# A data-dependent branch that is not taken: at the tail of an expert stage, or behind the first products of its tenth pair

## The chip, the cores and the metric

The kernel runs on one core of a Trainium2 chip. The metric is the device time of one execution in microseconds (us), as a median over runs. The engines named below are PE (TensorE: matmuls, and PEld, its weight loads), ACT (ScalarE), DVE (VectorE), POOL (GpSimd) and SP (SyncE, which here issues the large DMA transfers). Each has its own instruction stream and is synchronized with the others by semaphores. Times on the trace count from the first instruction.

## The reference

Two blocks are run one after the other over 256 tokens of width 1024. The second block has two layers, and each layer ends in a mixture of experts, the place of this change: 32 experts in four groups, two experts chosen for each token.

```
def second_block(x, ...):
    h = layer_norm(x, ln_in_g, ln_in_b)
    for i in range(DEPTH):                      # DEPTH = 2
        mix = hybrid_mixer(h, ...)
        h = layer_norm(DEEPNORM_ALPHA * h + mix, ln1_g[i], ln1_b[i])
        ffn = hierarchical_moe(h, ...)
        h = layer_norm(DEEPNORM_ALPHA * h + ffn, ln2_g[i], ln2_b[i])
    return h

# in grouped_expert_mlp, for each token's two experts e, with gate weight g:
#   y += g * ((silu(x @ w_gate[e]) * (x @ w_up[e])) @ w_down[e])
```

## The kernel before

`moe()` computes the expert stage of one layer. The weights of all 32 experts are read whatever the routing, and each expert has 64 slots (`CAP`) into which its tokens are gathered. The experts are taken in 16 pairs. A loop over `st` from 0 to 17 runs the pairs as a pipeline: at `st` come the gate and up products of pair `st` (`first_products`, L1793), the additions of pair `st-2` into the output's accumulators (`combine`, L1834, in two halves), the transposes of pair `st-1` (`turned`, L1810, evicted by ACT at L1812), the gating of pair `st` (`gated`, L1802 and L1803), on odd `st` the gathering of the tokens of the next pairs (`gather`, L1700 to L1734), and the down products of pair `st-1` (`second_products`, L1820, evicted at L1823 and L1824).

The weights come in 96 transfers of 2 MB a layer, two each for gate, up and down of a pair, into ten places. All stand on SP's queue, in the order of their use; transfer n reuses the place of transfer n-10 and so waits until PE has read that one. Two of the ten places are made of two halves (L1554), one for each expert of the pair; the others are one transfer (L1544).

An expert could be chosen by more tokens than it has slots. The largest count of a layer stands in `mxi` (tile `e_kept`, written before the loop). Every engine loads it into a register (`values_load`, L1856) and jumps over the body of `overflow()` if the count is no larger than 64 (`tc.If`, L1857). With the inputs here it is not larger in either layer: the body is skipped in both. The body's instructions stand in every engine's stream between the compare and the code after it. PE's order is written by hand: the loop's order is kept on PE (`manual_schedule`), and this is interrupted around the branch. The order of the other engines is found by the scheduler, which moves nothing across the branch.

Of the kernel before, what the change touches and what calls it, by code (L numbers as in the profile page):

```python
# [19 lines left out]
S = 256  # L20
# [680 lines left out]
def row_of(k, cols):  # L701

    b = k.t(k.work, [P, D], "row", bufs=3)
    for h in range(2):
        p = k.ps(tag="m3")
        for j in range(4):
            c = 4 * h + j
            k.nc.tensor.matmul(p[:, j * P:(j + 1) * P], cols[:, c:c + 1].to_broadcast([P, P]), k.ident,
                               start=True, stop=True)
        k.nc.scalar.activation(b[:, h * 512:(h + 1) * 512], p, AF.Copy)  # L710
    return b
# [781 lines left out]
CAP = 64  # L1493
NE = 32

EW = (("ew0", 3), ("ew1", 6))

NX, SPLIT = 10, 6
# [2 lines left out]
def moe(k, l, h, hsum, rows, const, cc):  # L1501


    nc, tc, a, W, A = k.nc, k.tc, k.a, k.work, k.act
# [3 lines left out]

    view = {n: k.t(W, [P, m, 2048], n) for n, m in EW}
    view["hx"] = k.t(k.const, [P, 10, 1024], "hl", F32, 1).rearrange("p (a b) c -> p a (b c)", b=2)  # L1510
# [46 lines left out]
    def prefetch(n):  # L1557
        while nxt[0] < min(n, len(order)):
            fetch(nxt[0], (1,) if nxt[0] == SPLIT else (0, 1))
            nxt[0] += 1  # L1560
            if nxt[0] == SPLIT - 2:
                fetch(SPLIT, (0,))
        if n >= len(order):

            while later:
                nc.sync.dma_start(*later.pop(0))
# [8 lines left out]
    G, pos = (kept[:, o:o + 64].rearrange("p (t e) -> p t e", t=NT) for o in (0, 64))  # L1575
# [3 lines left out]
    hH, hL = (k.t(k.act, [P, NT, D], f"e_{n}", F32R) for n in "hl")  # L1579
# [3 lines left out]
    for t in range(NT):  # L1583
# [3 lines left out]
        last = nc.vector.scalar_tensor_tensor(hc[:, t], h[:, t], mean, rows[0], op0=OP.add, op1=OP.mult).ins  # L1587
# [31 lines left out]
    def low_parts(t, after):  # L1619
        with tc.issue_after(after):  # L1620
            return nc.vector.tensor_tensor(hL[:, t], hc[:, t], hH[:, t].bitcast(F32), op=OP.subtract).ins
# [8 lines left out]
    acc = k.acc()  # L1630

    def residual(src, i):
        for t in range(NT):
            for hf in range(2):
                nc.tensor.matmul(acc[t][hf], al[:, i], src[:, t, hf * 512:(hf + 1) * 512],
                                 start=src is hH and i == 0, stop=False)
# [42 lines left out]
    last = low_parts(0, nc.vector.tensor_tensor(v(M), v(M), og4, op=OP.mult).ins)  # L1679
# [9 lines left out]
    sh = k.t(A, [P, 2, 512], "e_sh")  # L1689
# [77 lines left out]
    mxi = kept[:, 128:129].bitcast(I32)  # L1767
# [11 lines left out]
    last = NE // 2 - 1  # L1779

    def first_products(pr, xg, between=None):
        es = (2 * pr, 2 * pr + 1)
        gu = []
        for nm in ("gate", "up"):
            p = k.ps(tag="aux")
            for q in range(2):
                prefetch(index[nm, q, pr] + NX)
                if q and between:
                    between()
                    between = None  # L1790
                for kk, i in steps:
                    o = (es[i] % 4) * CAP
                    nc.tensor.matmul(p[64 * i:64 * i + 64], xg[:, 4 * q + kk, o:o + CAP], tiles[nm, q, pr](i, kk),  # L1793
                                     start=(q == 0 and kk == 0), stop=(q == 1 and kk == 3))
            gu.append(p)
            if pr == 0 and nm == "gate":
                next(first)
        return gu

    def gated(pr, gate, up):  # L1800
        s_ = sh[:, 0]
        nc.scalar.activation(s_, gate, AF.Silu)  # L1802
        i = nc.vector.scalar_tensor_tensor(s_, s_, at[pr][1], up, op0=OP.mult, op1=OP.mult)  # L1803
        k.anchor = s_[:, :1]
        return i.ins

    def turned():
        p = k.ps([P, 4, P], "m3")
        for f in range(4):
            nc.tensor.transpose(p[:, f], sh[:, 0, f * P:(f + 1) * P], k.ident)  # L1810
        hh = sh[:, 1].rearrange("p (f c) -> p f c", f=4)
        nc.scalar.activation(hh, p, AF.Copy)  # L1812
        return hh

    def second_products(pr, hh):
        for hf in range(2):
            p = k.ps(tag="m3")
            prefetch(index["down", hf, pr] + NX)
            for f, i in steps:
                nc.tensor.matmul(p[64 * i:64 * i + 64], hh[:, f, 64 * i:64 * i + 64],  # L1820
                                 tiles["down", hf, pr](i, f), start=f == 0, stop=f == 3)
            yh, yl = ys[:, 2 * hf], ys[:, 2 * hf + 1]
            nc.scalar.activation(yh, p, AF.Copy)  # L1823
            nc.vector.tensor_tensor(yl, p, yh.bitcast(F32), op=OP.subtract)  # L1824

    def combine(pr, hf):
        if pr == -1 and hf == 1:
            residual(hL, 0)
        if pr < 0:
            return  # L1830
        sT, _ = at[pr]
        for t in range(NT):
            for q in range(2):
                nc.tensor.matmul(acc[t][hf], sT[:, t * P:(t + 1) * P], ys[:, 2 * hf + q], start=False, stop=pr == last and q == 1)  # L1834

    ordered = ExitStack()
    ordered.enter_context(tc.manual_schedule(engines={mybir.EngineType.PE}))
    for st in range(last + 3):
        if st <= last:
            gu = first_products(st, xg, (lambda: next(first)) if st == 0 else None)  # L1840
        combine(st - 2, 0)
        if 1 <= st <= last + 1:
            hh = turned()
        if st <= last:
            done = gated(st, *gu)
        combine(st - 2, 1)
        if st % 2 and st < last:
            xg, *_ = gather(st + 1, done)
        if st == last:
            rows = [row_of(k, cc[:, o:o + KD]) for o in (C2.off["out_g"][0], C2.off["out_b"][0])]  # L1850
        if 1 <= st <= last + 1:
            second_products(st - 1, hh)
        if st == last:

            ordered.close()
            cnt = nc.values_load(mxi[0:1, 0:1], min_val=0, max_val=S)  # L1856
            with tc.If(cnt > k.cap):  # L1857
                overflow(k, l, acc, hH, hL, pos, G, const, sh[:, 1])
            ordered.enter_context(tc.manual_schedule(engines={mybir.EngineType.PE}))
    ordered.close()  # L1860
    return acc, rows

# [78 lines left out]
def tile_two_blocks(tc, a, out):  # L1941
    with ExitStack() as ctx:
# [17 lines left out]
        for l in range(L):  # L1960
            k.phase = f"_m{l}"
            o, _ = C2.off["in_b"]
            if l:
                x = k.t(k.const, [P, NT, D], "x")
            normed = ln_T(k, acc if l else row_halves(x), x, after, k.c2[:, l, o:o + KD], None if l else gain)
            hsum = k.t(k.work, [P, NT, 2], "hsum")
            mixer(k, l, normed, x, hsum, const, k.c2[:, l])
            k.phase = f"_e{l}"
            acc, after = moe(k, l, x, hsum, rows(2 + 2 * l), const, k.c2[:, l])
# [35 lines left out]
```

## Time and profile before

| what | value |
|---|---|
| median of 3 runs (lowest to highest) | 1907.97 us (1903.83 to 1912.17) |
| the profiled execution's own time | 1917.61 us |
| its span, first to last instruction | 1915.9 us |
| mean granted TensorE clock | 0.973 |
| PE busy | 1800.3 us (94% of the span) |
| DMA, mean | 283 GB/s |

The profile is of one execution; its span and 1.7 us around it make its time, which is 9.6 us above the median. The two expert stages fill most of the slices 17 to 26 and 31 to 40 of the 40 into which the page cuts the span; between them and ahead of them stand mixers and the first block.

### The profile page before, as it was taken

The numbers are of one execution on the slowest core, as the hardware profiler recorded it, in microseconds if no ns is written. First come the engines' busy times: TensorE is split into PE (matmuls) and PEld (weight loads), VectorE is DVE, ScalarE is ACT, GpSimd is POOL, SyncE is SP. The second block draws the span as 40 slices with busy tenths as digits, with TensorE's granted clock in tenths as the row PEclk, the third lists the DMA queues.
The fourth block names the chain that finished last, engine by engine and source line by source line (L and its number), as shares of the span: only waits on it lengthen the run. The fifth ranks groups of instructions, "written<-read, shape, count | busy, mean of one in ns | idle before, by whom it ended". The sixth has DMA issues, their size and how long they took to land. (4 is left out here: it accounts for less than half of the span.)

```text
span 1915.9 us, 29809 instructions
## 1 busy us (share of the span) xinstructions
PE 1800.3 (94%) x12598; PEld 1227.4 (64%) x12598; DVE 771.4 (40%) x1495; ACT 594.7 (31%) x1022; POOL 126.1 (7%) x255
## 2 busy tenths in 40 slices
PE   7999999999999999999999999788999999999996
PEld 7889998889998888744443443377885444434333
DVE  4754545655556858711111111157784111111012
ACT  4554445554444635211110110145442111111011
POOL 1100000010010310100000000012110000000000
PEclk9999999999999979999999999997999999999998
DMA  6335564235554416799999999941278999999995
GB/s 251 111 135 193 178 210 151 89 129 202 185 200 163 138 46 258 285 411 426 427 427 426 427 427 426 381 169 68 90 298 367 427 426 426 427 426 426 427 426 207
DMA packets 55105, 541.63 MB, mean 283 GB/s; under 512 B 6448, under 2 KB 6960, under 8 KB 10928
## 3 DMA queue, kind: packets, MB, share of 16 engines
q1 hardware_dynamic: 52352, 531.19, 68.9%
q0 software_dynamic: 2320, 8.24, 1.4%
q8 instruction: 104, 1.70, 0.4%
q14 instruction: 41, 0.34, 0.0%
q10 hardware_dynamic: 288, 0.15, 0.0%
HBM read 538.52 MB, written 1.05 MB: 282 GB/s over the span
## 5 line engine op out<-in xcount | busy, mean ns | idle before, releaser
L161 DVE TENSOR_TENSOR hl<-w,hl 128x1024 fp32r<-128x1024 f32 (+2 forms) x252 | 295.7, 1183 | 225.6 <-ACT hl L159 223.1
L159 ACT ACTIVATE hl<-w 128x1024 fp32r<-128x1024 f32 (+2 forms) x252 | 256.4, 1026 | 286.8 <-PE aux L129 106.5
L1793 PE MATMUL aux<-ew_e,XG_e 128*64 128x512 f32 x992 | 243.5, 600 | 7.8 <-DMA ew_e<-in_moe_up 5.0
L1803 DVE SCALAR_TENSOR_TENSOR e_sh_e<-e_sh_e,e_kept_e,aux 128x512 f32<-128x512 f32 x32 | 23.9, 747 | 492.2 <-ACT e_sh_e L1802 482.2
L1793 PEld LDWEIGHTS aux<-ew_e,XG_e 128*64 128x64 f32 x992 | 77.2, 139 | 164.5 <-issue 149.4
L1812 ACT ACTIVATE e_sh_e<-m 128x512 f32<-128x512 f32 x32 | 19.2, 599 | 492.8 <-PE m L1810 492.8
L1793 PE MATMUL aux<-hl,XG_e 128*64 128x512 f32 x480 | 127.7, 594 | 10.1 <-DVE e_y_e L1824 5.7
L129 PE MATMUL aux<-hl_f,hl 128*128 128x256 f32 x1056 | 131.5, 284 | 0.6 <-DVE hl_f L245 0.3
L1824 DVE TENSOR_TENSOR e_y_e<-m,e_y_e 128x512 fp32r<-128x512 f32 x64 | 44.2, 691 | 217.3 <-ACT e_y_e L1823 214.6
L129 PEld LDWEIGHTS aux<-hl_f,hl 128*128 128x128 f32 x1056 | 129.7, 192 | 2.8 <-DVE hl_f L245 0.7
L129 PE MATMUL m<-hl_f,hl 128*128 128x256 f32 x1056 | 130.3, 283 | 0.0
L129 PEld LDWEIGHTS m<-hl_f,hl 128*128 128x128 f32 x1056 | 128.3, 192 | 0.0
L182 PE MATMUL mm<-hl,m_f 128*128 128x512 f32 x528 | 123.5, 390 | 0.0
L1820 PE MATMUL m<-ew_e,e_sh_e 128*64 128x512 f32 x432 | 107.4, 596 | 3.5 <-DVE e_y_e L1824 2.8
L182 PEld LDWEIGHTS mm<-hl,m_f 128*128 128x128 f32 x528 | 97.9, 188 | 19.5
L1823 ACT ACTIVATE e_y_e<-m 128x512 fp32r<-128x512 f32 x64 | 38.2, 598 | 204.9 <-PE m L1820 204.9
L1793 PE MATMUL aux<-w,XG_e 128*64 128x512 f32 x384 | 84.6, 593 | 2.8 <-DVE e_y_e L1824 2.8
L1834 PE MATMUL mm<-e_y_e,slots_e 128*128 128x512 f32 x256 | 78.3, 429 | 9.2 <-issue 5.7
L1793 PEld LDWEIGHTS aux<-hl,XG_e 128*64 128x64 f32 x480 | 40.4, 137 | 67.1 <-issue 54.3
L129 PE MATMUL aux<-hl_m,hl 128*128 128x256 f32 (+1 forms) x576 | 77.6, 291 | 1.7 <-ACT hl_m L782 0.8
L1717 PE MATMUL m<-e_y_e,e_h_e 128*128 128x256 f32 x256 | 56.5, 300 | 22.5 <-DVE e_y_e L1700 22.5
L1820 PEld LDWEIGHTS m<-ew_e,e_sh_e 128*64 128x64 f32 x432 | 32.4, 137 | 65.8 <-issue 57.1
(571 smaller groups left out, 2639.1 us busy)
## 6 DMA issues: line engine op xcount, KB each, us to landing
ew_e<-in_moe_gate SPq DMA_DIRECT2D x28, 2048.0 KB, 28.8
ew_e<-in_moe_up SPq DMA_DIRECT2D x28, 2048.0 KB, 23.3
ew_e<-in_moe_down SPq DMA_DIRECT2D x24, 2048.0 KB, 29.4
w<-in_w_gate_up SPq DMA_DIRECT2D x44, 1024.0 KB, 4.9
w<-in_w_in SPq DMA_DIRECT2D x36, 1024.0 KB, 5.0
w<-in_moe_down SPq DMA_DIRECT2D x14, 2048.0 KB, 26.4
w<-in_moe_gate SPq DMA_DIRECT2D x12, 2048.0 KB, 24.1
hl<-in_moe_up SPq DMA_DIRECT2D x12, 2048.0 KB, 26.8
```

What stands on the lines that cost most here:

```text
L129: self.nc.tensor.matmul(out, x, y, start=(i == 0 and j == 0), stop=(i == n - 1 and j == len(terms) - 1))
L159: nc.scalar.activation(vo(hv), s, AF.Copy)
L161: nc.vector.tensor_tensor(vo(lv), s, vo(hv).bitcast(F32), op=OP.subtract)
L182: self.nc.tensor.matmul(acc[t][h], u1, u2, start=(kg == 0 and q == 0), stop=(kg == n_k - 1 and q == len(terms) - 1))
L1717: nc.tensor.matmul(p[:, j], src[:, t, c], sel[t], start=n == 0, stop=n == 3)
L1793: nc.tensor.matmul(p[64 * i:64 * i + 64], xg[:, 4 * q + kk, o:o + CAP], tiles[nm, q, pr](i, kk), start=(q == 0 and kk == 0), stop=(q == 1 ...
L1803: i = nc.vector.scalar_tensor_tensor(s_, s_, at[pr][1], up, op0=OP.mult, op1=OP.mult)
L1812: nc.scalar.activation(hh, p, AF.Copy)
L1820: nc.tensor.matmul(p[64 * i:64 * i + 64], hh[:, f, 64 * i:64 * i + 64], tiles["down", hf, pr](i, f), start=f == 0, stop=f == 3)
L1823: nc.scalar.activation(yh, p, AF.Copy)
L1824: nc.vector.tensor_tensor(yl, p, yh.bitcast(F32), op=OP.subtract)
L1834: nc.tensor.matmul(acc[t][hf], sT[:, t * P:(t + 1) * P], ys[:, 2 * hf + q], start=False, stop=pr == last and q == 1)
```

## The change

The load of the count and the branch move from the end of the step at which `st` is 15 (behind `second_products(14)`) to the step at which `st` is 9, between `first_products(9)` and `combine(7, 0)`. A constant `LATE = 9` names the step. All else in the source is the same; lines below it move down by two.

```
+LATE = 9
...
         if st <= last:
             gu = first_products(st, xg, (lambda: next(first)) if st == 0 else None)
+        if st == LATE:
+
+            ordered.close()
+            cnt = nc.values_load(mxi[0:1, 0:1], min_val=0, max_val=S)
+            with tc.If(cnt > k.cap):
+                overflow(k, l, acc, hH, hL, pos, G, const, sh[:, 1])
+            ordered.enter_context(tc.manual_schedule(engines={mybir.EngineType.PE}))
         combine(st - 2, 0)
...
         if 1 <= st <= last + 1:
             second_products(st - 1, hh)
-        if st == last:
-
-            ordered.close()
-            cnt = nc.values_load(mxi[0:1, 0:1], min_val=0, max_val=S)
-            with tc.If(cnt > k.cap):
-                overflow(k, l, acc, hH, hL, pos, G, const, sh[:, 1])
-            ordered.enter_context(tc.manual_schedule(engines={mybir.EngineType.PE}))
     ordered.close()
```

PE's order before, in the first of the two layers, near the end of the stage (`mm` are the output's accumulators, `m` other PSUM tiles; between the two pieces stands the body of the branch):

```order
L1820 MATMUL m_895_9574<-ew_e_705_7683,e_sh_e_745_7841 64x512 x8
L1820 MATMUL m_896_9585<-ew_e_705_7683,e_sh_e_745_7841 64x512 x8
L1856 TENSOR_LOAD e_kept_e_708_7701
L1857 COMPARE_AND_BRANCH
...
L1857 UNCONDITIONAL_BRANCH
L1834 MATMUL mm_7795<-e_y_e_746_7842,slots_e_729_7791 128x512 x2
L1834 MATMUL mm_7797<-e_y_e_746_7842,slots_e_729_7791 128x512 x2
L1810 MATMUL m_925_9986<-const_69,e_sh_e_745_7841 128x128 x4
L1834 MATMUL mm_7796<-e_y_e_746_7842,slots_e_729_7791 128x512 x2
L1834 MATMUL mm_7798<-e_y_e_746_7842,slots_e_729_7791 128x512 x2
L1820 MATMUL m_926_9996<-w_67,e_sh_e_745_7841 64x512 x8
```

The load and the compare stood between the down products of pair 14 and what is left for pair 15. PE's order of the changed kernel in the same layer, at the tenth pair (`aux` are the gate and up products):

```order
L1795 MATMUL aux_8847<-ew_e_705_7683,XG_e_821_8686 64x512 x16
L1795 MATMUL aux_8866<-w_67,XG_e_821_8686 64x512 x16
L1846 TENSOR_LOAD e_kept_e_708_7701
L1847 COMPARE_AND_BRANCH
...
L1847 UNCONDITIONAL_BRANCH
L1836 MATMUL mm_7795<-e_y_e_746_7842,slots_e_729_7791 128x512 x2
L1836 MATMUL mm_7797<-e_y_e_746_7842,slots_e_729_7791 128x512 x2
L1812 MATMUL m_865_9275<-const_69,e_sh_e_745_7841 128x128 x4
L1836 MATMUL mm_7796<-e_y_e_746_7842,slots_e_729_7791 128x512 x2
L1836 MATMUL mm_7798<-e_y_e_746_7842,slots_e_729_7791 128x512 x2
L1719 MATMUL m_867_9290<-e_y_e_746_7842,e_h_e_709_7706 128x256 x2
```

They now stand behind the 32 products of pair 9's up and ahead of the combine of pair 7; the matmuls themselves keep their order. SP's queue before, in the same layer, around the transfers of that step:

```order
L1544 DMA w_67<-in_moe_up 128x4096 x2
L1554 DMA ew_e_704_7682<-in_moe_down 128x2048
L1554 DMA hl_7684<-in_moe_down 128x2048
L1544 DMA hl_7684<-in_moe_down 128x4096
L1544 DMA hl_7684<-in_moe_gate 128x4096
L1554 DMA x_7898<-in_moe_gate 128x2048
L1554 DMA xw_7901<-in_moe_gate 128x2048
L1544 DMA ew_e_704_7682<-in_moe_up 128x4096
```

And SP's queue in the changed kernel:

```order
L1546 DMA w_67<-in_moe_up 128x4096 x2
L1556 DMA ew_e_704_7682<-in_moe_down 128x2048
L1546 DMA hl_7684<-in_moe_down 128x4096
L1846 TENSOR_LOAD e_kept_e_708_7701
L1847 COMPARE_AND_BRANCH
...
L1847 UNCONDITIONAL_BRANCH
L1556 DMA hl_7684<-in_moe_down 128x2048
L1546 DMA hl_7684<-in_moe_gate 128x4096
L1556 DMA x_7898<-in_moe_gate 128x2048
L1546 DMA ew_e_704_7682<-in_moe_up 128x4096
L1556 DMA xw_7901<-in_moe_gate 128x2048
```

SP's branch stands behind the second transfer of the down weights of pair 8, with all later transfers behind it, and the second half of a place made of halves now follows the whole transfer that it led before. The same holds for both layers, and in each for five such halves from here on.

## Rows read from the trace of the kernel before

**Rows 1.** The page's span in 40 slices: DMA busy tenths and rate.

```profile
DMA  6335564235554416799999999941278999999995
GB/s 251 111 135 193 178 210 151 89 129 202 185 200 163 138 46 258 285 411 426 427 427 426 427 427 426 381 169 68 90 298 367 427 426 426 427 426 426 427 426 207
```

**Rows 2.** The page's DMA issues: size and median time from issue to landing.

```profile
ew_e<-in_moe_gate SPq DMA_DIRECT2D x28, 2048.0 KB, 28.8
```

**Rows 3.** Timeline of PE, first layer's tail: start, length, count, idle before, releaser.

```profile
1222.01 3.65 PE L1793 MATMUL aux<-ew_e,XG_e 128*64 128x512 f32 x16 [1.25 <-DMA ew_e<-in_moe_up]
1225.59 1.20 PE L1834 MATMUL mm<-e_y_e,slots_e 128*128 128x512 f32 x4
...
1226.98 1.18 PE L1834 MATMUL mm<-e_y_e,slots_e 128*128 128x512 f32 x4
...
1231.74 7.09 PE L1820 MATMUL m<-ew_e,e_sh_e 128*64 128x512 f32 x32
1244.53 2.08 PE L1834 MATMUL mm<-e_y_e,slots_e 128*128 128x512 f32 x4 [5.70 <-issue]
...
1249.10 7.55 PE L1820 MATMUL m<-w,e_sh_e 128*64 128x512 f32 x32
```

**Rows 4.** Timeline of PE, second layer's tail.

```profile
1881.15 7.09 PE L1820 MATMUL m<-ew_e,e_sh_e 128*64 128x512 f32 x32
1890.37 1.15 PE L1834 MATMUL mm<-e_y_e,slots_e 128*128 128x512 f32 x4 [2.13 <-PEq L1857]
...
1893.85 7.73 PE L1820 MATMUL m<-w,e_sh_e 128*64 128x512 f32 x32
```

**Rows 5.** Windows at the tails: busy time by engine, granted PE clock, DMA share, GB/s.

```profile
1243.00:1246.00 3.00, 1.47 (x4) 1.19 (x5) 0.00 (x0) 0.00 (x0) 0.00 (x0) 0.54 0.00 0
1246.00:1250.00 4.00, 4.00 (x12) 2.34 (x12) 0.00 (x0) 0.60 (x1) 0.00 (x0) 0.50 0.02 6
...
1892.00:1896.00 4.00, 4.00 (x13) 1.81 (x14) 0.00 (x0) 0.60 (x1) 0.00 (x0) 0.60 0.02 4
```

**Rows 6.** The branch's line by queue: duration in ns (min/median/max), first and last start.

```profile
L1857 SPq COMPARE_BRANCH  x2: 50/52/53, 1208.8 to 1857.7; - x2
...
L1857 PEldq COMPARE_BRANCH  x2: 5985/6170/6356, 1235.0 to 1884.2; - x2
...
L1857 PEldq EVENT_SEMAPHORE  x2: 51/51/51, 1241.4 to 1890.3; - x2
```

**Rows 7.** The page's DMA queue of PE's instructions: packets, MB, share.

```profile
q8 instruction: 104, 1.70, 0.4%
```

**Rows 8.** Timeline of PE at the tenth pair, first layer.

```profile
1047.85 7.04 PE L1793 MATMUL aux<-w,XG_e 128*64 128x512 f32 x32
1054.82 1.21 PE L1834 MATMUL mm<-e_y_e,slots_e 128*128 128x512 f32 x4
...
1058.91 0.63 PE L1717 MATMUL m<-e_y_e,e_h_e 128*128 128x256 f32 x2 [1.52 <-DVE e_y_e L1700]
```

**Rows 9.** PE's waits, 1054 to 1240 us: total, times, longest.

```profile
PE aux L1793 <- DMA ew_e<-in_moe_up: 2.5, 2, 1.3
PE aux L1793 <- DMA hl<-in_moe_up: 1.3, 1, 1.3
PE aux L1793 <- DMA hl<-in_moe_gate: 0.6, 1, 0.6
```

**Rows 10.** The same, second layer, 1704 to 1890 us, behind an equal first row.

```profile
PE aux L1793 <- DMA hl<-in_moe_up: 1.4, 1, 1.4
PE aux L1793 <- DMA hl<-in_moe_gate: 1.1, 1, 1.1
```

**Rows 11.** Timeline of SP's queue at the tenth pair, first layer: issues.

```profile
1010.86 3.76 SPq L1544 DMA_DIRECT2D w<-in_moe_up  x2
...
1021.16 0.33 SPq L1544 DMA_DIRECT2D hl<-in_moe_down  x1
```

## The prediction

> **What bounds the kernel now.** I read the page's slices first. In the two expert stages the DMA engines are full and move 425 to 427 GB/s [rows 1]. A 2 MB transfer (2,097,152 bytes) at 427 GB/s takes 4.9 us, so weights land at that pace whatever PE does, as long as SP's queue stays ahead. It does: a transfer lands 28.8 us after its issue [rows 2], so about six (28.8 / 4.9) are under way. PE is nearly as slow as the weights. At the tenth pair it is behind them: the first up transfer, issued at 1010.86 [rows 11], lands at about 1010.86 + 28.8 = 1039.7, and PE turns to it at 1047.85 [rows 8], 8 us later. Towards the stage's end PE has caught up and waits for weights, the last time 1.25 us at 1222.01 [rows 3]. The list of PE's waits from the tenth pair to the branch shows what that comes to: 2.5 + 1.3 + 0.6 = 4.4 us in the first layer [rows 9] and 2.5 (an equal row) + 1.4 + 1.1 = 5.0 us in the second [rows 9, 10]. This is slack: a delay of PE at the tenth pair is given back out of it, because PE would otherwise stand and wait.
>
> At the tail there is no slack left. The weights of the last pair are landing (DMA share 0.00 from 1243 us on [rows 5]), and nothing but PE's chain is left: combine, transposes, combine, down products, then the layer norm. What PE loses there is lost.
>
> Now the branch. PE's compare lasts 6.0 and 6.4 us, while SP's, for the same test, lasts 0.05 us [rows 6]. The compares start at 1235.0 and 1884.2, while PE still works off what was queued ahead of them: the down products end at 1231.74 + 7.09 = 1238.83 [rows 3] and 1881.15 + 7.09 = 1888.24 [rows 4]. So about 4 us of each are hidden. The rest shows as idle time of 5.70 us and 2.13 us ahead of the combine [rows 3, 4]. Behind each gap the granted clock is 0.50 to 0.60 for some microseconds [rows 5], half the full 2.4 GHz for most of that time.
>
> A page of the Trainium skill, "Advanced Engine Details and Errata", section Control Flow Timing, gives about 108 ns for a compare-and-branch. SP's row is of that order; PE's is sixty times that. By that figure the gaps at the tails would not be the branch's, and the move would take nothing away; that is the fourth rival, and the trace speaks against it.
>
> **What the old place costs, and the move saves.** The undisturbed pattern is one step earlier: from the combine's start at 1225.59 to the second combine's end at 1226.98 + 1.18 = 1228.16 are 2.6 us [rows 3]. Put behind the end of the down products of pair 14:
> First layer: the last down products start at 1238.83 + 2.6 = 1241.4 instead of 1249.10, 7.7 us earlier, and take 7.09 instead of 7.55 us at full clock [rows 3]: 7.7 + 0.5 = 8.2 us.
> Second layer: 1888.24 + 2.6 = 1890.8 instead of 1893.85, 3.0 us, and 7.09 instead of 7.73 us [rows 4], 0.6: together 3.7 us (3.65 rounded).
> Sum: 11.9 us. For all of it to arrive, the last weights must be there in time. DMA is silent after 1243 [rows 5], the second half of the last down products would start at 1241.4 + 3.5 = 1244.9, and so it is not held. If it were, by a microsecond or two, the gain falls by as much.
>
> **What the new place costs.** The branch comes behind 32 matmuls of 7.04 us [rows 8], as it came behind 32 of 7.09 us, so PE's queue covers the same 4 us of the compare. DMA is as busy, so the fetch of the jump's target has the same traffic beside it. The nearest rows give two prices. By the second layer's tail: 2.1 us idle, then 1893.85 - 1890.37 = 3.5 us instead of 2.6 for the combines, and 0.6 on the products behind: 2.1 + 0.9 + 0.6 = 3.6 us. By the first layer's: 5.7 idle, 1249.10 - 1244.53 = 4.6 instead of 2.6, and 0.5: 5.7 + 2.0 + 0.5 = 8.2 us.
> Which one? In the second layer PE resumes as the compare's closing semaphore event starts (1890.3, then 1890.37 [rows 4, 6]). In the first that event is at 1241.4 and PE resumes only at 1244.53 [rows 3, 6]: 3.1 us more, a second stop. PE's instructions arrive in packets of 1.70 MB / 104 = 16 KB [rows 7], so I read it as a landing close to a packet's end, where the next packet must be awaited as well. Counting instructions in both streams, I find neither new place near such an end; the count is an estimate. I take 3.6 us for both layers and keep 8.2 as the bound. Nothing is an unlikely lower bound, as the skipped body is as long as before.
> 3.6 us is less than 4.4 and 5.0 us of slack, so the new place costs the stage nothing, and its last weights still meet a waiting PE. Without that cover it would be 2 x 3.6 = 7.2 us.
>
> **The other engines.** ACT, DVE and POOL meet the branch while PE is inside the first products of pair 9; ACT's and DVE's next work needs PE's output, so this is hidden. SP meets it ahead of time: its last issue before it is the whole transfer that stood at 1021.16 [rows 11], some 34 us before PE reaches the branch. All later weights are queued behind it, with about 29 us of transfers under way. SP's compare of 0.05 us is nothing against that; even one like PE's, 6 us, would only make the flights shorter. The five halves that now follow a whole transfer land up to 4.9 us later. PE, 8 us behind plus 3.6, has passed that at the tenth pair. Where it has caught up it might wait, but out of the same slack, so at most 4.9 - 4.4 = 0.5 us is lost.
> A new wait: PE's transposes behind the branch wait for all transfers that SP issued ahead of its branch, the gather's evictions too. The last of them lands near 1021.16 + 28.8 = 1050; PE is there at 1054.82 + 1.2 + 2.1 = 1058. There are 8 us to spare.
>
> **The sum.** 11.9 - 0 = 11.9 us. The profiled execution of 1917.61 us would be 1905.7. It is 9.6 us above the median, and no row says that its tails cost more than in other executions, so I take the same from the median: 1907.97 - 11.9 = 1896.1, faster by 0.62%.
>
> **The rivals.**
> 1. The new place costs the first layer's price. Then 8.2 - 4.4 = 3.8 us in the first layer or 8.2 - 5.0 = 3.2 us in the second are not given back: with one layer 1896.1 + 3.5 = 1899.6, with both 1903.1. For it: one of two rows is of that price. Against: the second stop is seen once, and the count.
> 2. The slack isn't usable or the clock stays low longer, since a wait of 1.52 us follows closely at 1058.91 [rows 8]; up to the 7.2 us of the uncovered price is lost: about 1900 to 1903. The 1.52 us is a wait for DVE's work on this very pair and moves with the delay.
> 3. Slower. If PE's transposes waited for all transfers under way and not only for those ahead of SP's branch, each layer would stop for 29 us and lose 29 + 3.6 - 4.7 = 28: 1907.97 + 56 - 11.9 = 1952. It decides from a hold of about 12 us a layer: 2 x (12 + 3.6 - 4.7) - 11.9 = 10 us. Against it stands SP's queue, where the branch is two transfers behind the up weights that PE is reading.
> 4. No change: the gaps have another cause than the branch. 1908. Against: the idle ends within 0.1 us of the compare's end in the second layer [rows 4, 6].
>
> **Chances and range.** The forecast has 0.62, rival 1 has 0.18, rival 2 0.1, rival 3 0.05, rival 4 0.05. The likeliest case's own range is 1892 to 1900, as the runs shown lie 4 us to either side of their median. The other faster cases reach 1903, and with such a spread about 1905; below, 1890. So 1890 to 1905. About 0.5%, 9.5 us, is what a measurement of this kernel can tell from no change. That is 1898.4, close to the forecast: of its 0.62 three quarters lie beyond, and of rivals 1 and 2 a third: 0.46 + 0.09 = 0.55 faster. Slower is rival 3, 0.05. The rest, 0.40, is within.
>
> **What the profile after would show.** At both tails the combine follows the down products without idle time, the last down products take 7.1 us, and the clock stays at 1.0. At the tenth pair a compare of about 6 us on PE's queue, an idle time near 2 us ahead of the combine, and a stretch of half clock. PE's waits for weights behind it fall by 3 to 4 us a layer, and the last wait for up weights is still there, near 1222 us in the first layer. DMA stays full throughout. Wrong it would be with an idle time of over 5 us there, with waits of the transposes on transfers, with a gap in the weights' pace, or with tails that wait for something else.

## The result, and the profile after

The changed kernel took 1886.41 us (median of 4 runs, 1880.74 to 1889.88) against 1907.03 us for the kernel before (4 runs, 1903.83 to 1912.17): a ratio of 0.9891, with a 95% interval of 0.9855 to 0.9927. That is faster, as forecast, but 20.6 us instead of 11.9, and below the lower end of the range. Later runs, told below, put the difference lower: over all runs of the two kernels except one of the kernel before, which took 2987 us at a mean granted clock of 0.55, the changed kernel's mean is 1887.9 us (22 runs), that of before 1904.6 us (79 runs), 16.7 us apart with a 95% interval of 2.6 us to either side. The profiled execution of the changed kernel is the one of 1889.88 us, with a span of 1888.2 us.

The expert stage shows what was forecast for the tails. PE's timeline of the changed kernel at the first layer's tail, answering [rows 3] (start, length, work, count; no row has idle time before it), and at the second's, answering [rows 4]:

```profile
1217.03 7.09 PE L1822 MATMUL m<-ew_e,e_sh_e 128*64 128x512 f32 x32
1224.05 1.19 PE L1836 MATMUL mm<-e_y_e,slots_e 128*128 128x512 f32 x4
1226.54 7.09 PE L1822 MATMUL m<-w,e_sh_e 128*64 128x512 f32 x32
1233.55 1.43 PE L1836 MATMUL mm<-e_y_e,slots_e 128*128 128x512 f32 x5
...
1857.21 7.09 PE L1822 MATMUL m<-ew_e,e_sh_e 128*64 128x512 f32 x32
1873.72 1.42 PE L1836 MATMUL mm<-e_y_e,slots_e 128*128 128x512 f32 x5
```

The kernel before had its last combines at these two places in its timeline:

```profile
1256.58 1.42 PE L1834 MATMUL mm<-e_y_e,slots_e 128*128 128x512 f32 x5
...
1901.51 1.45 PE L1834 MATMUL mm<-e_y_e,slots_e 128*128 128x512 f32 x5
```

From the start of the down products of pair 14 to that of the last combine it was 1256.58 - 1231.74 = 24.84 us, and is 1233.55 - 1217.03 = 16.52 us: 8.3 us saved in the first layer. In the second 1901.51 - 1881.15 = 20.36 us became 1873.72 - 1857.21 = 16.51 us: 3.85 us saved. The forecast said 8.2 and 3.7.

At the new place, PE's timeline of the changed kernel (idle time and releaser in brackets), answering [rows 8], with the start of pair 9's up products, the combine behind the branch in each layer, and the first down product of pair 8:

```profile
1032.47 7.04 PE L1795 MATMUL aux<-w,XG_e 128*64 128x512 f32 x32
1042.07 1.17 PE L1836 MATMUL mm<-e_y_e,slots_e 128*128 128x512 f32 x4 [2.56 <-PEq L1847]
1052.80 0.64 PE L1822 MATMUL m<-ew_e,e_sh_e 128*64 128x512 f32 x1
...
1672.60 7.04 PE L1795 MATMUL aux<-w,XG_e 128*64 128x512 f32 x32
1682.18 2.05 PE L1836 MATMUL mm<-e_y_e,slots_e 128*128 128x512 f32 x4 [2.54 <-PEq L1847]
```

Windows of the changed kernel (busy time of PE, PEld, DVE, ACT, POOL, then granted clock, DMA share, GB/s) at the new place and at the old, answering [rows 5]:

```profile
1042.00:1046.00 4.00, 3.39 (x12) 2.18 (x12) 1.05 (x3) 1.09 (x2) 0.00 (x0) 0.69 1.04 434
1046.00:1050.00 4.00, 3.82 (x17) 3.85 (x18) 0.37 (x2) 0.60 (x1) 0.00 (x0) 0.50 0.99 416
1224.00:1227.00 3.00, 3.00 (x16) 2.03 (x16) 0.69 (x1) 1.20 (x2) 0.00 (x0) 1.00 0.56 227
```

The branch's line on PE's queue, after, answering [rows 6] (ns, first and last start):

```profile
L1847 PEldq COMPARE_BRANCH  x2: 6249/6280/6312, 1035.7 to 1675.6; - x2
```

The compare still takes PE 6.3 us, its uncovered rest is 2.5 us, and half clock now stands behind it here; at the tail the clock is 1.00. Whether this is hidden is read from the whole way. From the start of pair 9's up products to that of pair 14's down products it was 1231.74 - 1047.85 = 183.89 us and is 1217.03 - 1032.47 = 184.56; in the second layer, where those up products of the kernel before stand in its timeline as

```profile
1697.16 7.04 PE L1793 MATMUL aux<-w,XG_e 128*64 128x512 f32 x32
```

it was 1881.15 - 1697.16 = 183.99 and is 1857.21 - 1672.60 = 184.61. So 0.7 and 0.6 us of the new place are not hidden. Executions differ by nearly as much: in the first layer this way takes 183.6 to 184.4 us in the six profiles with the branch at the tail, and 183.9 to 185.3 us in the five with it here and nothing that stops PE twice. The two terms are rough.

PE's waits behind the new place, after, first layer, answering [rows 9] (total us, times, longest):

```profile
PE aux L1795 <- DMA ew_e<-in_moe_up: 3.0, 2, 1.8
PE aux L1795 <- DVE e_y_e L1826: 1.4, 1, 1.4
PE aux L1795 <- DMA hl<-in_moe_gate: 0.7, 1, 0.7
```

The waits of these products for weights fall from 5.0 us (the 4.4 of [rows 9] and two rows of 0.4 and 0.2) to 3.7, in the second layer from 5.6 to 4.5. The forecast said 3 to 4 us a layer. One of two waits of 1.4 us for DVE is gone too, in either layer. So the delay is given back, but only a part of it out of the listed waits for weights.

The stages give 8.3 + 3.85 - 0.7 - 0.6 = 10.9 us. The forecast's sum was 11.9. What else came has to be outside these ways.

One gain of over 4 us stands where the prediction did not look: in the second layer's mixer, right behind the first layer's expert stage. PE's timeline there, before:

```profile
1298.13 1.05 PE L969 MATMUL mm<-x_early_m,r_sq_m 128*128 128x2 f32 x8 [1.64 <-ACT r_sq_m L957]
1306.02 0.22 PE L996 MATMUL m<-const,x_sm_m 8*128 8x8 f32 x1 [2.70 <-ACT x_sm_m L991]
```

The same work after, without these waits of 1.64 + 2.70 = 4.3 us:

```profile
1273.40 0.95 PE L969 MATMUL mm<-x_early_m,r_sq_m 128*128 128x2 f32 x8
1278.46 0.29 PE L996 MATMUL m<-const,x_sm_m 8*128 8x8 f32 x2
```

Over the whole stretch, from the products of `r_lr` (L917) to the transposes of `r_v` (L1115), PE takes 26.2 us before and 21.6 after. In the four profiles with the first layer's branch at the old place and this mixer unaltered it is 26.2 to 26.7 us, in the eight with that branch moved or left out 21.6 to 21.7. The rest of the mixer, up to the second layer's first products, differs more than that between executions of one kernel: 148.7 and 155.7 us in two profiles of before, 147.4 to 152.7 in three of after. In the first two profiles it takes the gain back (148.7 and 152.7), so it is the stretch that shows it, and not the mixer as a whole.

ACT is late there because of one small transfer, and this one because of POOL. Timelines of POOL and ACT of the kernel before:

```profile
1281.78 1.47 POOL L114 COPY r_roz_m<-r_lr_m 128x1 f32<-128x1 f32 x2 [0.37 <-issue]
1283.51 0.61 POOL L116 DMA_DIRECT2D x_small_m<-in_a_log  x1
...
1289.48 1.28 ACT L1010 ACT_TABLE_LOAD   x1 [5.38 <-DMA x_small_m<-in_a_log]
```

The copies' line by queue in that stretch, before (ns, first and last start):

```profile
L114 POOLq EVENT_SEMAPHORE  x9: 43/43/43, 1281.0 to 1281.7; - x9
L114 POOL COPY r_roz_m<-r_lr_m x2: 332/766/1200, 1281.8 to 1282.9; 128x1 f32<-128x1 f32 x2
```

The timelines of POOL and ACT of the changed kernel:

```profile
1258.41 0.30 POOL L114 COPY r_roz_m<-r_lr_m 128x1 f32<-128x1 f32 x2
1258.77 0.61 POOL L116 DMA_DIRECT2D x_small_m<-in_a_log  x1
...
1261.63 1.28 ACT L1010 ACT_TABLE_LOAD   x1 [0.46 <-DMA x_small_m<-in_a_log]
```

Before, nine semaphore waits stand among these copies, six of them in a row ahead of the first copy to `r_roz`, and then that copy took 1.2 us; the load of `a_log` (a row of 8 numbers for each partition) was issued behind it, and ACT waited 5.4 us for it. After, the two copies take 0.30 us together, and ACT waits 0.46 us. From the first of the copies to the load's issue it was 1283.51 - 1280.99 = 2.5 us and is 0.7; from the issue to the landing 5.9 us and 2.8.

### The profile page after: what moved, and what is told of

The parts are those of the page before. It is cut to its first block, busy times and chain, and to the rows that moved or that the text cites. A ratio compares the mean times of both kernels' runs of the same rounds, so it can differ in the third digit from the quotient of the medians.

```text
span 1888.2 us, 29832 instructions
## 1 busy us (share of the span) xinstructions
PE 1783.8 (94%) x12598; PEld 1217.5 (64%) x12598; DVE 770.2 (41%) x1495; ACT 594.7 (31%) x1022; POOL 124.5 (7%) x255
## 3 DMA queue, kind: packets, MB, share of 16 engines
q8 instruction: 103, 1.69, 0.4%
## 5 line engine op out<-in xcount | busy, mean ns | idle before, releaser
L161 DVE TENSOR_TENSOR hl<-w,hl 128x1024 fp32r<-128x1024 f32 (+2 forms) x252 | 295.6, 1182 | 222.7 <-ACT hl L159 220.1
L1805 DVE SCALAR_TENSOR_TENSOR e_sh_e<-e_sh_e,e_kept_e,aux 128x512 f32<-128x512 f32 x32 | 23.9, 747 | 492.6 <-ACT e_sh_e L1804 482.6
L1719 PE MATMUL m<-e_y_e,e_h_e 128*128 128x256 f32 x256 | 57.1, 304 | 21.7 <-DVE e_y_e L1702 21.7
## 6 DMA issues: line engine op xcount, KB each, us to landing
ew_e<-in_moe_up SPq DMA_DIRECT2D x28, 2048.0 KB, 22.9
```

Source lines behind the costliest of these rows:

```text
L161: nc.vector.tensor_tensor(vo(lv), s, vo(hv).bitcast(F32), op=OP.subtract)
L1719: nc.tensor.matmul(p[:, j], src[:, t, c], sel[t], start=n == 0, stop=n == 3)
```

## The experiments

The expectations speak of three theories. A: all that the move gives is what the tails lose, some 11 to 12 us, and the rest of the first difference is chance of the executions. B: the move gives something systematic ahead of the first expert stage too, where the two first profiles differ most. C, formed from the traces: the tails, and the second layer's mixer through POOL. The ratios are against the runs of the kernel before on the same chip, with 95% intervals.

**The two kernels again.** No edit. First the kernel before:

> The kernel before, unaltered, against itself: the ratio has to hold 1. What it is for is a second profile of the kernel before. Theory A: in another execution the stretches with a low granted clock ahead of the first expert stage lie elsewhere or are gone (0.84 at 40 to 60 us, 0.75 and 0.57 at 660 to 700 us in the first profile), and the first expert stage begins up to 15 us earlier. Theory B: they are there again at the same places, and the tails alone differ from the changed kernel by 11 to 12 us.

1905.28 us (12 runs), 1.001 [0.9988, 1.0032]. Then the changed kernel:

> The changed kernel again, unaltered, timed against the kernel before. Measured at first: 20.6 us faster at the medians, where the tails account for 8.0 us in the first layer and about 3 us in the second. Theory A: the move is worth those 11 to 12 us, and the rest is the clock that was granted in the mixers, which differs from one execution to the next; then the ratio comes out near 0.994 this time, and the stretch up to the first expert stage (696 us before, 681 us after in the two profiles) is no longer shorter by 15 us. Theory B: something that the move changes ahead of the first expert stage is worth the other 9 us; then the ratio is again near 0.989 and the same stretch is short again.

1886.25 us (12 runs) against 1903.11, 0.9927 [0.9901, 0.9953], and in another set of runs:

> The changed kernel once more, unaltered, to narrow its ratio to the kernel before. By the stages of the traces the move is worth 11.5 to 12 us, a ratio of 0.9938. Theory A (the rest of the first measurement was the clock granted in the mixers by chance): 0.993 to 0.995, and over all runs the means differ by 11 to 14 us. Theory B (the change also helps elsewhere): again 0.989 to 0.991, and means that differ by 16 to 20 us.

1886.02 us (6 runs) against 1905.21, 0.9913 [0.988, 0.9945]. By the expectations, 0.9913 and 16.7 us stand nearer to theory B (0.989 to 0.991, 16 to 20 us) than to A (11 to 14 us); the times do not decide, the traces do. In the first profile of before, the clock in the first layer's mixer was low; in the repeat it is that of the changed kernel, and the first expert stage starts as early. A window of 20 us in the first profile of before (last three numbers: granted clock, DMA share, GB/s):

```profile
660.00:680.00 20.00, 18.61 (x545) 13.41 (x545) 15.89 (x38) 8.71 (x26) 6.11 (x10) 0.75 0.17 57
```

The same window in its repeat:

```profile
660.00:680.00 20.00, 18.75 (x405) 13.89 (x395) 16.95 (x40) 8.12 (x25) 4.93 (x7) 0.91 0.04 13
```

And in the changed kernel:

```profile
660.00:680.00 20.00, 18.64 (x420) 13.98 (x409) 16.84 (x40) 8.16 (x26) 4.92 (x7) 0.91 0.05 18
```

So what lies ahead of the first stage differs between executions of one kernel: the stage's first products start at 805.8 and 790.1 us in the two profiles of before and at 790.4 to 794.5 in three of the changed kernel. Without a branch they start at 799.8. Nothing systematic shows there that theory B could rest on, though a difference of a microsecond or two would not be seen. Theory A had this part right.

**Without the branch.** The load of the count and the branch are left out, with the body of `overflow()`; with these inputs the body is never entered.

```
-        if st == LATE:
-            ordered.close()
...
-            ordered.enter_context(tc.manual_schedule(engines={mybir.EngineType.PE}))
```

> Load and branch left out in both layers, so the body for experts with more tokens than slots is left out (these inputs never enter it). If the new place is hidden behind PE's waits for weights, this is no faster than the changed kernel (within 2 us), though the idle time of about 2.5 us at the tenth pair is gone. If the new place costs its whole 3.6 us a layer, it is faster than the changed kernel by 7 us.

1883.63 us (6 runs), 0.9892 [0.9863, 0.9921]. PE's timeline of it, first layer: pair 9's up products, the first down product of pair 8, the last combine.

```profile
1040.40 7.04 PE L1795 MATMUL aux<-w,XG_e 128*64 128x512 f32 x32
1056.35 0.64 PE L1822 MATMUL m<-ew_e,e_sh_e 128*64 128x512 f32 x1
1241.24 1.42 PE L1836 MATMUL mm<-e_y_e,slots_e 128*128 128x512 f32 x5
```

The new place is priced by this. From up products to first down product are 1056.35 - 1040.40 = 15.95 us without a branch and 1052.80 - 1032.47 = 20.33 us in the changed kernel: the branch costs 4.4 us on the spot. To the last combine are 1241.24 - 1040.40 = 200.84 and 1233.55 - 1032.47 = 201.08 us: 0.2 us of the 4.4 are left at the end. In the second layer it is 3.9 us on the spot and again 0.2 at the end. So the expert stage hides a branch at this place. The times leave more open: 2.6 us below the changed kernel at the medians where at most 2 were expected, and 5.3 between the means, with some 5 us to either side.

**Cover taken away.** `LATE = 15`, the same branch behind the first products of the last pair.

```
-LATE = 9
+LATE = 15
```

> The changed kernel with the branch behind the first products of the sixteenth pair instead of the tenth. If it is PE's later waits for weights that hide the new place, nothing hides it here: the last gate and up weights have been read. Each layer then pays the 3.6 us (idle of 2.1 to 2.6 us ahead of a combine, half clock behind it) on the chain that ends the stage, so 7 us more than the changed kernel and some 5 us less than before; 3 us more if a target falls on a packet's end. If a branch costs nothing as long as it stands behind first products, whatever the place, the time is that of the changed kernel.

1896.33 us (8 runs) against 1905.64, 0.9943 [0.9921, 0.9966]; 10 us above the changed kernel by the medians, 7.7 by the means, where 7 were expected. PE's timeline, first layer:

```profile
1032.28 7.04 PE L1795 MATMUL aux<-w,XG_e 128*64 128x512 f32 x32
1214.11 1.25 PE L1836 MATMUL mm<-e_y_e,slots_e 128*128 128x512 f32 x4 [3.58 <-PEq L1847]
1238.25 1.43 PE L1836 MATMUL mm<-e_y_e,slots_e 128*128 128x512 f32 x5
```

1238.25 - 1032.28 = 205.97 us, 4.9 us more than after (in the second layer 4.5). The price is a little above that at the tenth pair (3.58 us idle against 2.56), and here no slack returns it: 9.4 us in both layers. So it is the place, and not a cheaper branch, that makes the move pay.

**The second stop.** The forecast read the first layer's long gap in the kernel before as a jump to a target near the end of a packet of instructions. Transposes put into the body that is never entered shift what stands behind it: one in the kernel before, 14, 15 and 30 in the changed one.

```
-            for f in range(4):
+            for f in (0,) * 1 + (0, 1, 2, 3):
```

> The kernel before with one more transpose, repeated, in the body of the branch, which is never entered: no executed instruction differs, only the place of the code after the branch in PE's instruction stream. If the second stop of 3.1 us at the first layer's tail comes from a target at the very end of an instruction packet, it goes: idle ahead of the combine 2.1 to 2.6 us instead of 5.7, and 3 to 5 us less in all (0.2%). If the second stop has another cause (a landing, a semaphore of another engine), the idle time stays at 5.7 us and the time is that of before.

1899.71 us (12 runs), 0.9981 [0.9953, 1.0008]: the time does not tell. The trace does: from the start of pair 14's down products to the end of the last combine the first layer takes 23.9 us, against 27.9 in the first profile of before, and the idle time of its combine, 5.70 us in [rows 3], is

```profile
1236.13 1.17 PE L1834 MATMUL mm<-e_y_e,slots_e 128*128 128x512 f32 x4 [2.60 <-PEq L1857]
```

The other way round, the changed kernel was to be given a second stop:

> The same with 14 more transposes: the code behind the first layer's branch begins some 13 instructions ahead of a packet's end by the same count. If the next packet is asked for only when the first has landed, PE resumes after 2.5 us of idle time, works off those 13 instructions in 1 to 2 us, and stops again for 1 to 2 us among the combine and the transposes. If the count is off by some instructions, this and the run with 15 differ from that by the place at which the second stop lies.

1886.67 us (1 run), idle time 2.78 us: no second stop.

> The changed kernel with 15 more transposes, repeated, in the body of the branch, which is never entered. By the count of instructions (12 of them for each transpose) the code behind the branch of the first layer moves from the middle of an instruction packet to its last instruction. Then the second stop comes back at the tenth pair of the first layer: idle of 5.5 to 6 us instead of 2.56 ahead of the combine or inside it, and the stage, which can hide some 5 us, ends 2 to 4 us later. The second layer stays at 2.1 to 2.6 us. If the second stop has nothing to do with packets, nothing changes.

1888.17 us (1 run), 2.55 us: none. These two missed, since 12 instructions had been counted for a transpose where the streams hold 6 (two for each of the body's three copies). 30 are the shift aimed at, 180 instructions:

> The changed kernel with 30 more transposes, repeated, in the body that is never entered. The runs with 14 and 15 showed that each moves the code behind it by 6 instructions and not by 12 (the next packet is asked for some 80 to 100 instructions earlier), so they had reached only half of the way. 30 times 6 are 180, the number of instructions by which the change moved the branch forward in the stream, counted in packets of 256: the code behind the first layer's branch then stands at the same place in a packet as before the change. If a target at a packet's end makes the second stop, the first layer's tenth pair idles 5.5 to 6 us ahead of the combine (2.56 in the changed kernel), the second layer stays at 2.1 to 2.6, and the first stage, which can hide some 5 us, ends 2 to 4 us later. If not, 2.5 us in both.

1885.93 us (1 run). PE's timeline of it:

```profile
1032.20 7.04 PE L1795 MATMUL aux<-w,XG_e 128*64 128x512 f32 x32
1047.50 2.08 PE L1836 MATMUL mm<-e_y_e,slots_e 128*128 128x512 f32 x4 [8.27 <-issue]
1059.44 0.64 PE L1822 MATMUL m<-ew_e,e_sh_e 128*64 128x512 f32 x1
1234.79 1.42 PE L1836 MATMUL mm<-e_y_e,slots_e 128*128 128x512 f32 x5
```

The second stop is there: where the target stands in the stream decides. The packets of PE's instruction queue in the traces show why. Behind each of the 26 compares in the profiles a packet of 16 KB starts 3.5 to 4.0 us after the compare does and takes about 1.1 us, and PE goes on 1.4 to 1.7 us after its end. A second packet comes before PE's first matmul in six cases: the first layer with the branch at its old place and no transposes added (five profiles), and this one. In [rows 3] the second ends at 1243.10 us and PE resumes at 1244.53; here it ends at 1046.09 and PE resumes at 1047.50.

It is 5.7 us more idle time, and with half clock behind it the branch costs 1059.44 - 1032.20 - 15.95 = 11.3 us on the spot. Yet the way to the last combine is 1234.79 - 1032.20 = 202.59 us, only 1.5 us longer than after. So the slack at the tenth pair holds some 9 to 10 us, twice what I read from the waits for weights. Part of it shows in the list of PE's waits behind that place (total us, times, longest), without the branch:

```profile
PE aux L1795 <- DMA ew_e<-in_moe_up: 3.4, 2, 2.2
PE aux L1795 <- DVE e_y_e L1826: 2.8, 2, 1.4
PE aux L1795 <- DMA hl<-in_moe_up: 1.3, 1, 1.3
```

The same list with 30 transposes:

```profile
PE aux L1795 <- DVE e_y_e L1826: 1.4, 1, 1.4
PE aux L1795 <- DMA ew_e<-in_moe_up: 0.6, 1, 0.6
```

The waits for weights fall from 5.6 us (3.4 and 1.3 in these rows, and three rows of 0.2 to 0.4) to 0.6, and one of two waits of 1.4 us for DVE is gone: 6.4 us. Some 3 us more lie in the same products, in no row of the list: from start to start, the 384 gate and up products behind the place take 91.8 us without the branch and 83.9 with 30 transposes, 7.9 us less, where the list's rows of weights give 5.0.

**The mixer.** Only the second layer's branch is moved, in the changed kernel:

```
-        if st == LATE:
+        if st == LATE and l == 1:
...
+        if st == last and l == 0:
```

> The branch moved in the second layer only; the first layer keeps it at the tail. By the stages, the second layer's tail is 3.8 us shorter (from the last down products of pair 14 to the last combine), the first layer's tail stays at 16 to 17 us where the changed kernel has 8.6, and, by theory C, the second mixer still has the long wait for a_log (over 5 us on ACT) and the stretch of about 10 us on PE, since that hangs on the first layer's branch. By theory A the stretch can come out at 5.3 here as well.

1901.94 us (1 run); one run tells little of the time. ACT's row is that of before:

```profile
1273.91 1.28 ACT L1010 ACT_TABLE_LOAD   x1 [5.36 <-DMA x_small_m<-in_a_log]
```

So the first layer's branch sets this wait and the second's does not. In every profile with the first layer's branch at the old place, where nothing else was changed in the mixer, the wait is between 5.36 and 5.83 us (four profiles); in those with the branch elsewhere or left out it is 0.45 to 0.69 us (eight). To see what triggers it, one copy that touches the memory of `r_roz` earlier was added to the kernel before, with the branch at its old place:

```
-        t = k.late(T(shape, tag))
+        t = k.late(pre[tag] if tag in pre else T(shape, tag))
...
+    if l:
+        pre["r_roz0"] = k.late(T([P, 2, S], "r_roz0"), anchor=gq[:, :1])
```

> The branch stays at its old place, the a_log transfer too. In the kernel before, the first instruction of POOL in the second mixer that touches memory used by the branch's body (the first column of r_roz) waits for some 20 semaphores, nine instructions, and the copy itself then takes 1.2 us instead of 0.18, beside a DVE instruction. Here one more copy of POOL, a microsecond earlier, touches that memory first, so the waits come ahead of the load of a_log's chain. If the list of waits, by pushing POOL's copy into DVE's work, makes the transfer late, POOL issues it as early as in the changed kernel (0.7 us behind the first of its copies, not 2.5) and ACT waits under 1.5 us for it. If the transfer is late for another reason, ACT's wait stays at 5 us or more.

1905.76 us (1 run). POOL's semaphore waits (by queue), its timeline and ACT's:

```profile
L114 POOLq EVENT_SEMAPHORE  x10: 17/43/43, 1263.1 to 1263.9; - x10
...
1274.34 0.18 POOL L114 COPY r_roz_m<-g_q_m 128x1 f32<-128x1 f32 x1 [11.03 <-ACT g_q_m L911]
1276.09 0.61 POOL L116 DMA_DIRECT2D x_small_m<-in_a_log  x1
...
1278.96 1.28 ACT L1014 ACT_TABLE_LOAD   x1 [0.46 <-DMA x_small_m<-in_a_log]
```

The added copy takes the waits, 11 us ahead of itself while POOL is idle, and ACT's wait is 0.46 us with the branch where it was; PE's stretch is 21.6 us. In the changed kernel a list of seven such waits stands ahead of an instruction of the layer norm, while POOL works on the one before it:

```profile
L252 POOLq EVENT_SEMAPHORE  x7: 43/43/43, 1237.8 to 1238.4; - x7
```

Without a branch there is no such list. The other half, the late load, was taken away by loading `a_log` with the first small loads of the mixer:

```
+           (alog, a["a_log"][l:l + 1].broadcast_to([P, 8])),
...
-    k.late(small, (alog, a["a_log"][l:l + 1].broadcast_to([P, 8])))
```

> The branch stays at its old place. In the second layer's mixer of the kernel before, ACT waits 5.4 to 5.8 us for a small transfer (a_log, 4 KB) that POOL issues there, in the changed kernel 0.46 us; PE is 4.6 us longer from the products of the narrow slab to the transposes of what ACT makes of them. Here that transfer is issued with the other small loads, ahead of the branch, as all of it is needed only in the mixer. Theory C (the transfer's lateness is worth the 4.6 us that the tails don't account for): ACT waits for it no longer, the stretch is 5.3 us instead of 9.8 to 10.3, and the time is some 4 to 5 us below before (0.2%), the tails unchanged. Theory A (chance): the stretch stays at about 10.

1900.53 us (10 runs) against 1906.89, 0.999 [0.9956, 1.0024]: the time does not tell 4 us here. In the trace PE's wait of 2.70 us is gone and that of 1.64 too, though the copy still takes its time; PE's stretch is 22.9 us, with a new wait of 1.16 us for DVE. Theory C stands for the mechanism: the first copies on POOL that touch memory of the branch's body catch up on the body's semaphores, and the load issued behind it is what ACT and PE wait for. Why the load then also lands late (5.9 us from issue, and ACT resumes 1289.48 - 1283.51 = 6.0 us behind it, against 1261.63 - 1258.77 = 2.9 us after) is open. DVE's L161 runs beside POOL's slow copy for 1.23 us, and the Trainium skill, "SBUF — State Buffer", section "SBUF: two separate sides", says that DVE and GpSimd share a pair of ports that one of them holds for a whole instruction. The slow copy would fit that; no run here took DVE's work away. The section also says that a transfer issued from GpSimd's queue waits for its descriptors while DVE runs an operation in a two-port mode. For L161 the traces do not bear that out: in the changed kernel it starts at 1258.79 us, beside the load's issue, and the load lands in 2.8 us. What stands beside the late load is DVE's L1100, which takes 2.5 us in the four profiles with the long wait and 0.7 in those with the short one; no run tells whether it holds up the load or is itself held up.

## Why the prediction was right in direction and wrong in size

**What bounds the kernel, and the old place.** Right. The tails gave 8.3 and 3.85 us against 8.2 and 3.7. The half clock behind the gap went with it.

**The new place.** The term was 3.6 us and measured 4.4 and 3.9; in the first layer the clock stays low for some 8 us, longer than I took from the second layer's tail. The choice against 8.2 was right, for the reason given: no packet's end stands at the target. The shifts by dead transposes and the packets show that this was the question, though my count of instructions for a transpose was off by half.

**The slack.** I set it at 4.4 and 5.0 us, the waits for weights. In the first layer it held 9 to 10 us in the run with the second stop, so rival 1 would have cost 1.5 us where I priced 3.8. Yet it may not return all: 0.7 and 0.6 us are missing against the kernel before, where I put nothing. Against the run without a branch only 0.2 are missing, and executions of one kernel differ by that much and more.

**The other engines.** This is the step that failed. I asked what the branch holds up at its new place, on ACT, DVE, POOL and SP, and not what it had held up behind its old one. Every engine has the branch, and I costed its removal on PE alone. On POOL its semaphores were paid by copies of the next mixer, 48 us behind POOL's compare, and PE lost 4.3 us there in waits, 4.6 over the stretch. The forecast's sum has nothing for this. The text ahead of the prediction says that the scheduler moves nothing across the branch; that is wrong for POOL, whose small loads for the next mixer come later in the program and stood ahead of the old branch (1229.3 to 1233.3 us, the compare at 1232.8). In the changed kernel the branch stands ahead of them (POOL's compare is at 788.7 us, the loads at 1214.6), and the semaphores are worked off before the next mixer, where they hold nothing up.

**The sum.** 8.3 + 3.85 - 0.7 - 0.6 + 4.3 = 15.2 us. All runs together show 16.7 us, 2.6 to either side. From 1907.03 these 15.2 would have given 1891.8, inside the range. Of the first result's further 5.4 us, 3.9 are chance of the executions, as the repeats show, and 1.5 lie within the interval; my range allowed 4.

**The rivals.** Rivals 3 and 4 are out: no transpose waits for transfers at the new place, and the gaps left with the branch. Rival 2 is out by the run without a branch.

## What to carry to other kernels

A branch that is never taken is work on every engine: look for what stands behind it on each queue, in the next stage too, before costing its move. Slack is better measured by a delay that is put in than by adding up the waits for one kind of transfer: here it held twice as much in the one layer where it was put in. Where two profiles differ far ahead of the change, run the same kernel again before explaining it.

## What was not expected of the hardware

PE's compare that jumps over a body takes 6.0 to 6.5 us in all 26 cases, while the other engines' takes 0.05 to 0.07 us. By the trace it is a wait for instructions: a packet of 16 KB of PE's instruction queue comes within it, and it ends 1.4 to 1.6 us after the packet does. If the target stands at a packet's end, 3.1 us more idle time come with it at the first layer's tail (5.70 against 2.60 us) and 5.7 at the tenth pair (8.27 against 2.56), where the second packet came later. The Trainium skill, "Runtime: NRT & Kernel Launch", section "Instruction fetch mechanics", says that instructions come in blocks of 16 KiB (256 instructions), and that a jump out of what is at hand must fetch before it goes on; the trace agrees in that 103 packets carry 1.69 MB, and that a shift of 180 instructions in the dead body makes the second stop. That six semaphore waits in a row, of 43 ns each, and a slow copy of 1.2 us on an otherwise idle engine could cost PE 4.3 us was the other surprise. What sets the clock in the mixers, which differed between executions of one kernel (0.75 and 0.91 in the same 20 us), stays open.
